# Last head's mean in full precision inside the output stage, and one unread full-precision matmul in the second layer's first feed-forward product

## The chip, the cores and the metric

The kernel runs on 1 core of a Trainium2 chip. The metric is the device time of one execution in microseconds. Before the change it is 868.81 us, the median of 3 runs (866.87 to 868.93).

## The reference

An encoder trunk of two layers works on 272 tokens (16 learned meta tokens and 256 given ones) of 1024 channels. Cut to what matters, one layer is:

```
u  = rms_norm(h)
q, k, v, g (retention), q, k, v (attention), gate_r, gate_a = split(u @ w_in)
r  = retention both ways, 8 heads of 128 values;
     per head: r / sqrt(mean(r*r) + 1e-6) * silu(g)      (r has its mean taken off)
y_r = r @ w_ret_o
y_a = windowed attention(q, k, v) @ w_att_o
h  = h + rms_norm((sigmoid(gate_r)*y_r + sigmoid(gate_a)*y_a) @ w_mix_o)
h  = h + rms_norm(square(relu(rms_norm(h) @ w_ff1)) @ w_ff2)
```

At the end the meta tokens are dropped. All of it is float32. The kernel computes a sigmoid as a tanh of half its argument, and 1/sqrt(x) as Exp(-0.5 Ln(x)) with one Newton step.

## The kernel before, in words

Channels lie on the 128 partitions and tokens on the free axis, so a product is 128 output channels by 272 tokens (layer 0) or 256 (layer 1, where the meta tokens' columns are no longer computed). `c0` is 0 or 16 for that. A product in float32 is made of three matmuls of a rounded type per 128 input channels (`mm3`, L135 to L138): high weights by high data, high by low, low by high. A full product (`product`, L146) is 8 such steps, 24 matmuls, into one bank of PSUM. The banks are named: three of tag a, two each of s and t, one of o. `wide()` (L85) deals out the tags in the rotation "asatats".

Weights arrive by DMA in units of 128 x 1024 (`unit`, L119). ScalarE copies a unit to its high part (L131), VectorE subtracts to get the low part (L132). 256 units pass through the kernel.

A layer runs in stages: the input projections; attention; retention; the attention output `att_o` (8 outputs of 4 steps, 12 matmuls each); the retention output `ret_o` (8 products); the mix (8 products) with a norm, `leave` (L296); the first feed-forward product `ff1` (32 products); the second. In layer 0 the second feed-forward product ends in `leave` too; layer 1 ends in a stage of its own, whose rows are normed in `scaled` (L834).

In the retention stage (L718 to L737) each head hh passes `similar` (decay weights by Exp, scores), `retained` (four full-precision instructions and a rounded one; a square on ScalarE; a split of the squares into high and low), and `normed` (L699): the mean of the squares over the head's 128 channels as two rounded matmuls with a matrix of 1/128 (`o128`, L702), then Ln, Exp (L705, L706), the Newton step, the gate, and a split into `rh` and `rl`, which `ret_o` reads. Between the heads' parts `fill(n)` puts n steps of the products gate_r and gate_a. Their results are added up on VectorE (`stt`, L92) into `thr` (one tile for all eight outputs) and `tha` (eight tiles). After the last head ScalarE computes the tanh of `thr` in one instruction of 8 x 256 elements and of `tha` in eight. `att_o` adds its results to 1 + tanh (tha) (L753), and `ret_o` to 1 + tanh(thr) in a similar manner.

The order of the instructions on each engine is made by the framework, which takes the code as traced and lists, engine by engine, what to issue next; the order in the code is a priority among those that are ready. Three means give the code a say. `tc.issue_after(x)` holds an instruction behind x where both are on one engine. `tc.keep_in_program_order(i)` holds i behind the instruction that was traced just before it on its engine. Tiles of a tag have a fixed number of buffers and wait for one. ScalarE computes Exp, Tanh and Ln from table sets: the compiler puts a table load before a function that isn't in the set loaded last, and `preload_act_table_set` (L207, L650, L743) loads a named set by hand.

The tanhs are held behind the last head's Exp:

```
        with tc.issue_after(last.ins):
            A.activation(thr[:, :, c0:], thr[:, :, c0:], AF.Tanh, scale=0.5)
            for x in tha:
                A.activation(x[:, c0:], x[:, c0:], AF.Tanh, scale=0.5)
        tc.keep_in_program_order(A.preload_act_table_set("natural_log_exp_and_others"))
```

`last` is the Exp of `normed(7)`. `mean` (L180) is a norm's mean over all 1024 channels, made of full-precision matmuls (L183) that take a float32 matrix as it is; `idle` is a 128 x 128 tile of zeros that `warm` (L175) uses.

Of the kernel before, what the change touches and what calls it, by code (L numbers as in the profile page):

```python
# [10 lines left out]
F32R = mybir.dt.float32r  # L11
F16 = mybir.dt.float16
BF16 = mybir.dt.bfloat16
AF = mybir.ActivationFunctionType
# [3 lines left out]
P = 128  # L18
# [4 lines left out]
T = SEQ + NM  # L23
# [18 lines left out]
def encoder(ctx: ExitStack, tc: tile.TileContext, order, w, h_in, gains, dec, decm, sink, sinkm, tabs, mats, esel, masks, rel, relm, grow, out):  # L42
    nc = tc.nc
    V, A, PE, G = nc.vector, nc.scalar, nc.tensor, nc.gpsimd
    mul, add, sub, mn = ALU.mult, ALU.add, ALU.subtract, ALU.min

    def pool(name, bufs=1, **kw):
        return ctx.enter_context(tc.tile_pool(name=name, bufs=bufs, **kw))
# [6 lines left out]
    four = pool("four", 4)  # L55
# [17 lines left out]
    def bank(tag, shape=None):  # L73
        t = psum.tile([P, 512], F32, tag=tag, name="ps_" + tag, bufs=BANKS[tag])
        if shape is None:
            return t
        n = int(np.prod(shape))
        v = t[:, :n]
        if len(shape) == 2:
            v = v.rearrange("p (a b) -> p a b", a=shape[0])  # L80
        elif len(shape) == 3:
            v = v.rearrange("p (a b c) -> p a b c", a=shape[0], b=shape[1])
        return v

    def wide():  # L85
        turn[0] += 1
        return "asatats"[turn[0] % 7]

    def f(t):
        return t.bitcast(F32)  # L90

    def stt(o, a, s, b, op0=mul, op1=mul):  # L92
        V.scalar_tensor_tensor(out=o, in0=a, scalar=s, in1=b, op0=op0, op1=op1)

    def split(xh, xl, x):
        A.activation(xh, x, AF.Copy)  # L96
        V.tensor_tensor(out=xl, in0=x, in1=f(xh), op=sub)  # L97

    def load(ap, dt=F32, name=None):
        t = const.tile(list(ap.shape), dt, name=name)  # L100
        nc.sync.dma_start(t, ap)
        return t
# [16 lines left out]
    def unit(*name):  # L119
        i = len(order)  # L120
        order.append(name)
        if not raws:
            list(fetch())
        raw, cuts = raws.pop(0)
        wh = ring.tile([P, D], F32R, tag="wh", name="wh")
        wl = ring.tile([P, D], F32R, tag="wl", name="wl")
        for c in cuts:
            with ExitStack() as later:
                for ins in held.get(i, ()):
                    later.enter_context(tc.issue_after(ins))  # L130
                A.activation(wh[:, c], raw[:, c], AF.Copy)  # L131
                V.tensor_tensor(out=wl[:, c], in0=raw[:, c], in1=f(wh[:, c]), op=sub)  # L132
        return wh, wl

    def mm3(ps, ah, al, bh, bl, first=True, last=True):  # L135
        PE.matmul(ps, ah, bh, start=first, stop=False)  # L136
        PE.matmul(ps, ah, bl, start=False, stop=False)  # L137
        return PE.matmul(ps, al, bh, start=False, stop=last)  # L138
# [3 lines left out]
    def flush():  # L142
        while deferred:
            deferred.pop(0)()

    def product(x, c0, tag, *name):  # L146
        wh, wl = unit(*name)
        ps = bank(tag, [T])
        for k in range(KD):
            sl = slice(k * P, (k + 1) * P)  # L150
            ins = mm3(ps[:, c0:], wh[:, sl], wl[:, sl], x[0][:, k, c0:], x[1][:, k, c0:], k == 0, k == KD - 1)
            if k == LAG and deferred:
                with tc.issue_after(ins.ins):
                    flush()
            yield ins, ps

    def proj(x, c0, tag, *name):
        for _, ps in product(x, c0, tag, *name):
            pass
        return ps  # L160
# [11 lines left out]
    idle = const.tile([P, P], F32, name="idle")  # L172
# [152 lines left out]
    mat = {}  # L325
# [37 lines left out]
    for l in range(DEPTH):  # L363
        c0 = 16 * l
        if l == 0:
            u, ss, early = lead()
        else:
            u, ss, _ = enter(l, 0, 0, update)
            early = [proj(u, 0, "asas"[i], "v_r", i) for i in range(4)]
        if l == 0:  # L370
            mat_sb = load(mats, name="mats")
            mat.update((n, mat_sb[:, i]) for i, n in enumerate(MATS))
            o128 = one.tile([P, P], F32R, tag="o128", name="o128")
# [124 lines left out]
        ao = tokens(5, "ao", (2, 4), 32 - c0)  # L498
# [3 lines left out]
        thr = slot(6, "thr")  # L502
# [46 lines left out]
        def behind():  # L549
            return tc.issue_after(anchor[0])  # L550
# [12 lines left out]
        if l == 0:  # L563
            ps = bank("s")
# [86 lines left out]
        tha = gate["gate_a"] = half("10a", "tha")  # L651
# [16 lines left out]
        sds, pos, pvs = {}, {}, {}  # L668
# [20 lines left out]
        def retained(hh):  # L689
            t = hh // 2  # L690
            po = pos[hh] = bank("ot"[hh % 2], [T])
            for c in range(2):
                PE.matmul(po[:, c0:], vr[:, c, hh * P:(hh + 1) * P], sds[hh][c][:, c0:], start=c == 0, stop=False)
            PE.matmul(po[:, c0:], vm[:, hh], tm[:, t, c0:], start=False, stop=True)
            sq = square(po[:, c0:], c0)
            pvs[hh] = four.tile([P, 2, T], F32R, tag="pt", name="sqs", bufs=3)
            split(*(pvs[hh][:, i, c0:] for i in range(2)), sq[:, c0:])

        def normed(hh):  # L699
            pv = bank("t", [T])  # L700
            for i in range(2):
                PE.matmul(pv[:, c0:], o128, pvs[hh][:, i, c0:], start=i == 0, stop=i == 1)  # L702
            y = two.tile([P, T], F32, tag="t1", name="vy")
            w2 = two.tile([P, T], F32, tag="t2", name="vw")
            A.activation(y[:, c0:], pv[:, c0:], AF.Ln, bias=eps)  # L705
            last = A.activation(y[:, c0:], y[:, c0:], AF.Exp, scale=-0.5)  # L706
            newton(w2[:, c0:], pv[:, c0:], 1e-6, y[:, c0:], w2[:, c0:])
            stt(w2[:, c0:], w2[:, c0:], -0.25, gt[:, hh, c0:])
            V.tensor_tensor(out=w2[:, c0:], in0=pos[hh][:, c0:], in1=w2[:, c0:], op=mul)
            split(rh[:, hh, c0:], rl[:, hh, c0:], w2[:, c0:])  # L710
            return last
# [6 lines left out]
        for hh in range(8):  # L718
            with behind():
                if hh < 7:  # L720
                    similar(hh + 1)
                retained(hh)
            fill(F[7])
            if hh == 0:
                for m in range(KD):
                    with tc.issue_after(ready.ins):
                        stt(gt[:, m, c0:], tg[:, m, c0:], 1.0, gt[:, m, c0:], op0=add)
                rh, rl = tokens(7, "rh", at=32 - c0), tokens(8, "rl", at=32 - c0)
            if hh % 2 and hh < 7:
                with behind():  # L730
                    meta((hh + 1) // 2)
            fill(F[6])
            with behind():
                last = normed(hh)
            fill(F[5])
        while queue or current:
            fill(1)  # L737

        with tc.issue_after(last.ins):
            A.activation(thr[:, :, c0:], thr[:, :, c0:], AF.Tanh, scale=0.5)  # L740
            for x in tha:
                A.activation(x[:, c0:], x[:, c0:], AF.Tanh, scale=0.5)
        tc.keep_in_program_order(A.preload_act_table_set("natural_log_exp_and_others"))  # L743

        for m2 in range(4):
            wh, wl = unit("att_o", m2)
            for i in range(2):
                m = 2 * m2 + i
                ps = bank(wide(), [T])
                for k in range(4):  # L750
                    sl = slice((4 * i + k) * P, (4 * i + k + 1) * P)
                    mm3(ps[:, c0:], wh[:, sl], wl[:, sl], ao[:, 0, k, c0:], ao[:, 1, k, c0:], k == 0, k == 3)
                stt(tha[m][:, c0:], tha[m][:, c0:], 1.0, ps[:, c0:], op0=add)  # L753

        z = tokens(2, "zh", at=32 - c0), tokens(3, "zl", at=32 - c0)
        for m in range(KD):
            ps = proj((rh, rl), c0, wide(), "ret_o", m)
# [16 lines left out]
        u, ss, accumulate = enter(l, 2, c0, update)  # L774
        fs, behind = [], []
# [8 lines left out]
        for m in range(KF):  # L784
            if m % KD == 0:
                a, b = ((5, 7), (8, 9), (6, 10), (2, 3))[m // KD]
                low = [tokens(i, "fl", (4,), 32 - c0) for i in ("10a", "10b")] if b == 10 else [tokens(b, "fl", at=32 - c0)]
                fs.append((rows(tokens(a, "fh", at=32 - c0)), sum(map(rows, low), [])))
            ps = proj(u, c0, wide(), "ff1", m)
            if l == 0 and 0 <= m - SUM < KD:  # L790
                accumulate(m - SUM)
            if l == 0 and m == SUM + KD:
                e2 = one.tile([P, T], F32, tag="rb", name="e2")
                A.activation(e2, mean([ss], c0), AF.Square, scale=8e-6 ** 0.5)
            behind.append((ps, fs[-1][0][m % KD][:, c0:], fs[-1][1][m % KD][:, c0:]))
            if len(behind) > BEHIND:
                squared(*behind.pop(0))
# [46 lines left out]
    for j in range(2):  # L844
# [22 lines left out]
        for i in range(2):  # L867
            sl = slice(j * 512, (j + 1) * 512)
# [6 lines left out]
    for i in range(2):  # L875
        for a, b in ((0, 512), (512, 768), (768, 1024)) if i else ((0, 512), (512, 1024)):
            sl = slice(a, b)
# [115 lines left out]
```

## Time and profile before

| what | value |
| --- | --- |
| median of 3 runs | 868.81 us (866.87 to 868.93) |
| profiled execution | 874.68 us |
| span of its trace | 872.9 us |
| mean granted TensorE clock | 0.996 |
| TensorE busy | 98% |
| VectorE busy | 70% |
| ScalarE busy | 65% |
| TensorE's share of the chain that ended last | 80% |
| VectorE's, ScalarE's share of it | 10%, 6% |

PE is TensorE's matmuls, PEld its weight loads, DVE VectorE, ACT ScalarE, POOL GpSimd and SP SyncE. The span is the time from the first to the last instruction; the profiled execution's own time has 1.8 us around it. The granted clock is a share of TensorE's full speed: 1.00 is 2.4 GHz and 0.50 is 1.2 GHz. Matmuls overlap: the duration of one (about 0.28 us) is longer than the step from its start to the start of the next, and the step is what counts. The chain that ended last is followed back from the last instruction to whatever released each.

### The profile page before, as it was taken

The numbers are of one execution on the slowest core, as the hardware profiler recorded it, in microseconds if no ns is written. First come the engines' busy times: TensorE is split into PE (matmuls) and PEld (weight loads), VectorE is DVE, ScalarE is ACT, GpSimd is POOL, SyncE is SP. The second block draws the span as 40 slices with busy tenths as digits, with TensorE's granted clock in tenths as the row PEclk, the third lists the DMA queues.
The fourth block names the chain that finished last, engine by engine and source line by source line (L and its number), as shares of the span: only waits on it lengthen the run. The fifth ranks groups of instructions, "written<-read, shape, count | busy, mean of one in ns | idle before, by whom it ended". The sixth has DMA issues, their size and how long they took to land.

```text
span 872.9 us, 16696 instructions
## 1 busy us (share of the span) xinstructions
PE 854.7 (98%) x6514; PEld 822.2 (94%) x6514; DVE 608.5 (70%) x1129; ACT 564.8 (65%) x1050; POOL 50.6 (6%) x114
## 2 busy tenths in 40 slices
PE   9999999999999999999999999999999999999997
PEld 8899999999989999999989999999999999998885
DVE  7889888878668555444468898888786775554544
ACT  7448788675558777544455578987845587783432
POOL 2112220000000000000000122200000000000000
PEclk9999999999999999999999999999999999999999
DMA  8544443446545655655635544434376276666661
GB/s 293 194 125 139 122 130 114 145 146 192 164 128 179 190 179 178 176 184 172 178 112 153 162 132 141 141 124 148 115 219 200 90 239 189 183 193 194 190 192 70
DMA packets 41407, 142.15 MB, mean 163 GB/s; under 512 B 5360, under 2 KB 6256, under 8 KB 41328
## 3 DMA queue, kind: packets, MB, share of 16 engines
q1 hardware_dynamic: 40896, 140.43, 52.3%
q8 instruction: 51, 0.84, 0.4%
q10 hardware_dynamic: 432, 0.66, 0.2%
q14 instruction: 28, 0.23, 0.1%
HBM read 140.02 MB, written 1.05 MB: 162 GB/s over the span
## 4 chain that ended last, share of the span: by engine, by line
PE 80%; DVE 10%; ACT 6%; issue 1%; DMA 1%; POOL 0%; SPq 0%; DVEq 0%; ACTq 0%; POOLq 0%
PE ps_a L136 12%; PE ps_a L137 12%; PE ps_a L138 12%; PE ps_s L138 5%; PE ps_s L136 5%; PE ps_s L137 5%; PE ps_t L136 4%; PE ps_t L137 4%; PE ps_t L138 4%; DVE wl L132 3%; PE ps_s L853 2%; PE ps_a L853 2%; PE ps_a L855 2%; PE ps_s L855 2%; PE ps_s L854 2%; PE ps_a L854 2%
## 5 line engine op out<-in xcount | busy, mean ns | idle before, releaser
L132 DVE TENSOR_TENSOR wl<-raw,wh 128x1024 fp32r<-128x1024 f32 x256 | 313.0, 1224 | 199.7 <-ACT wh L131 198.2
L131 ACT ACTIVATE wh<-raw 128x1024 fp32r<-128x1024 f32 x256 | 269.8, 1058 | 204.4 <-PE ps_a L137 62.3
L136 PE MATMUL ps_a<-uh,wh 128*128 128x272 f32 (+1 forms) x912 | 263.0, 289 | 2.8 <-ACT uh L242 2.8
L138 PE MATMUL ps_a<-uh,wl 128*128 128x272 f32 (+1 forms) x912 | 260.0, 285 | 0.5 <-DVE wl L132 0.3
L137 PE MATMUL ps_a<-ul,wh 128*128 128x272 f32 (+1 forms) x912 | 260.1, 286 | 0.0
L136 PEld LDWEIGHTS ps_a<-uh,wh 128*128 128x128 f32 x912 | 172.6, 189 | 3.8 <-ACT uh L242 3.2
L138 PEld LDWEIGHTS ps_a<-uh,wl 128*128 128x128 f32 x912 | 172.9, 190 | 1.2 <-DVE wl L132 0.8
L137 PEld LDWEIGHTS ps_a<-ul,wh 128*128 128x128 f32 x912 | 172.4, 189 | 0.4
L138 PE MATMUL ps_s<-uh,wl 128*128 128x272 f32 (+1 forms) x184 | 52.4, 285 | 0.3 <-DVE wl L132 0.3
L137 PE MATMUL ps_s<-ul,wh 128*128 128x272 f32 (+1 forms) x184 | 52.3, 284 | 0.0
L136 PE MATMUL ps_s<-uh,wh 128*128 128x272 f32 (+1 forms) x184 | 52.2, 284 | 0.0
L136 PE MATMUL ps_t<-uh,wh 128*128 128x272 f32 (+1 forms) x152 | 43.5, 286 | 1.3 <-ACT uh L242 1.3
L137 PE MATMUL ps_t<-ul,wh 128*128 128x272 f32 (+1 forms) x152 | 43.5, 286 | 0.0
L138 PE MATMUL ps_t<-uh,wl 128*128 128x272 f32 (+1 forms) x152 | 43.2, 284 | 0.0
L138 PEld LDWEIGHTS ps_s<-uh,wl 128*128 128x128 f32 x184 | 34.9, 190 | 0.5 <-DVE wl L132 0.5
L136 PEld LDWEIGHTS ps_s<-uh,wh 128*128 128x128 f32 x184 | 34.7, 189 | 0.0
L137 PEld LDWEIGHTS ps_s<-ul,wh 128*128 128x128 f32 x184 | 34.6, 188 | 0.0
L136 PEld LDWEIGHTS ps_t<-uh,wh 128*128 128x128 f32 x152 | 28.6, 188 | 1.5 <-ACT uh L242 1.5
L138 PEld LDWEIGHTS ps_t<-uh,wl 128*128 128x128 f32 x152 | 28.9, 190 | 0.0
L137 PEld LDWEIGHTS ps_t<-ul,wh 128*128 128x128 f32 x152 | 28.6, 188 | 0.1
L97 DVE TENSOR_TENSOR fl<-ft,fh 128x272 fp32r<-128x272 f32 (+1 forms) x64 | 27.6, 433 | 1.0 <-ACT fh L96 0.9
L96 ACT ACTIVATE fh<-ft 128x272 fp32r<-128x272 f32 (+1 forms) x64 | 27.2, 425 | 1.7
(311 smaller groups left out, 1963.5 us busy)
## 6 DMA issues: line engine op xcount, KB each, us to landing
raw<-in_w SPq DMA_DIRECT2D x256, 512.0 KB, 3.7
leads<-in_w SPq DMA_DIRECT2D x6, 256.0 KB, 5.6
tab<-in_tabs SPq DMA_DIRECT2D x2, 544.0 KB, 6.3
h<-in_h_in SPq DMA_DIRECT2D x3, 272.0 KB, 5.8
out<-yt SPq DMA_DIRECT2D x3, 256.0 KB, 2.1
leads<-in_w ACTq DMA_DIRECT2D x2, 256.0 KB, 3.4
gj<-in_grow SPq DMA_DIRECT2D x1, 512.0 KB, 4.7
mats<-in_mats SPq DMA_DIRECT2D x1, 320.0 KB, 7.2
```

The costliest lines, as they stand in the source:

```text
L96: A.activation(xh, x, AF.Copy)
L97: V.tensor_tensor(out=xl, in0=x, in1=f(xh), op=sub)
L131: A.activation(wh[:, c], raw[:, c], AF.Copy)
L132: V.tensor_tensor(out=wl[:, c], in0=raw[:, c], in1=f(wh[:, c]), op=sub)
L136: PE.matmul(ps, ah, bh, start=first, stop=False)
L137: PE.matmul(ps, ah, bl, start=False, stop=False)
L138: return PE.matmul(ps, al, bh, start=False, stop=last)
L853: PE.matmul(pss[i], xh, wh[:, sl], start=kk == 0, stop=False)
L854: PE.matmul(pss[i], xh, wl[:, sl], start=False, stop=False)
L855: PE.matmul(pss[i], xl, wh[:, sl], start=False, stop=kk == KF - 1)
```

## The change

It has six parts. For head 7 the squares aren't split, and the mean over them is one full-precision matmul (two instructions) with the float32 matrix `mat["o128"]`. `normed(7)` is taken out of the retention loop and traced in `att_o`, held behind the third matmul of step k = 1 of output 0; the tanhs of `tha` follow its Exp. `att_o` takes its banks from "asasa" and uses no bank of tag t. The tanh of `thr` is cut into three, for outputs 0 to 1, 2 to 4 and 5 to 7, traced behind the second, third and fourth unit of `att_o` and not held behind any instruction. The table preload is held behind the third of them. And in layer 1 a full-precision matmul of `idle` with 256 columns of the constant matrices goes to the bank of tag o, behind output 3 of `ff1`; nothing reads its result.

```diff
--- before.py
+++ after.py
@@ -693,13 +693,19 @@
                 PE.matmul(po[:, c0:], vr[:, c, hh * P:(hh + 1) * P], sds[hh][c][:, c0:], start=c == 0, stop=False)
             PE.matmul(po[:, c0:], vm[:, hh], tm[:, t, c0:], start=False, stop=True)
             sq = square(po[:, c0:], c0)
-            pvs[hh] = four.tile([P, 2, T], F32R, tag="pt", name="sqs", bufs=3)
-            split(*(pvs[hh][:, i, c0:] for i in range(2)), sq[:, c0:])
+            if hh == 7:
+                pvs[hh] = sq
+            else:
+                pvs[hh] = four.tile([P, 2, T], F32R, tag="pt", name="sqs", bufs=3)
+                split(*(pvs[hh][:, i, c0:] for i in range(2)), sq[:, c0:])
 
         def normed(hh):
             pv = bank("t", [T])
-            for i in range(2):
-                PE.matmul(pv[:, c0:], o128, pvs[hh][:, i, c0:], start=i == 0, stop=i == 1)
+            if hh == 7:
+                PE.matmul(pv[:, c0:], mat["o128"], pvs[hh][:, c0:], start=True, stop=True)
+            else:
+                for i in range(2):
+                    PE.matmul(pv[:, c0:], o128, pvs[hh][:, i, c0:], start=i == 0, stop=i == 1)
             y = two.tile([P, T], F32, tag="t1", name="vy")
             w2 = two.tile([P, T], F32, tag="t2", name="vw")
             A.activation(y[:, c0:], pv[:, c0:], AF.Ln, bias=eps)
@@ -730,27 +736,35 @@
                 with behind():
                     meta((hh + 1) // 2)
             fill(F[6])
-            with behind():
-                last = normed(hh)
+            if hh < 7:
+                with behind():
+                    normed(hh)
             fill(F[5])
         while queue or current:
             fill(1)
 
-        with tc.issue_after(last.ins):
-            A.activation(thr[:, :, c0:], thr[:, :, c0:], AF.Tanh, scale=0.5)
-            for x in tha:
-                A.activation(x[:, c0:], x[:, c0:], AF.Tanh, scale=0.5)
-        tc.keep_in_program_order(A.preload_act_table_set("natural_log_exp_and_others"))
+        def gates(ins):
+            with tc.issue_after(ins.ins):
+                last = normed(7)
+            with tc.issue_after(last.ins):
+                for x in tha:
+                    A.activation(x[:, c0:], x[:, c0:], AF.Tanh, scale=0.5)
 
         for m2 in range(4):
             wh, wl = unit("att_o", m2)
             for i in range(2):
                 m = 2 * m2 + i
-                ps = bank(wide(), [T])
+                ps = bank("asasa"[m % 5], [T])
                 for k in range(4):
                     sl = slice((4 * i + k) * P, (4 * i + k + 1) * P)
-                    mm3(ps[:, c0:], wh[:, sl], wl[:, sl], ao[:, 0, k, c0:], ao[:, 1, k, c0:], k == 0, k == 3)
+                    ins = mm3(ps[:, c0:], wh[:, sl], wl[:, sl], ao[:, 0, k, c0:], ao[:, 1, k, c0:], k == 0, k == 3)
+                    if m == 0 and k == 1:
+                        gates(ins)
                 stt(tha[m][:, c0:], tha[m][:, c0:], 1.0, ps[:, c0:], op0=add)
+            if m2:
+                x = thr[:, (0, 0, 2, 5)[m2]:(0, 2, 5, 8)[m2], c0:]
+                A.activation(x, x, AF.Tanh, scale=0.5)
+        tc.keep_in_program_order(A.preload_act_table_set("natural_log_exp_and_others"))
 
         z = tokens(2, "zh", at=32 - c0), tokens(3, "zl", at=32 - c0)
         for m in range(KD):
@@ -786,7 +800,11 @@
                 a, b = ((5, 7), (8, 9), (6, 10), (2, 3))[m // KD]
                 low = [tokens(i, "fl", (4,), 32 - c0) for i in ("10a", "10b")] if b == 10 else [tokens(b, "fl", at=32 - c0)]
                 fs.append((rows(tokens(a, "fh", at=32 - c0)), sum(map(rows, low), [])))
-            ps = proj(u, c0, wide(), "ff1", m)
+            for ins, ps in product(u, c0, wide(), "ff1", m):
+                pass
+            if l and m == 3:
+                with tc.issue_after(ins.ins):
+                    tc.keep_in_program_order(PE.matmul(bank("o", [T])[:, c0:], idle, mat_sb[:, 0:2].rearrange("p a b -> p (a b)"), start=True, stop=True))
             if l == 0 and 0 <= m - SUM < KD:
                 accumulate(m - SUM)
             if l == 0 and m == SUM + KD:
```

## Rows read from the trace of the kernel before

**Rows 1.** Busy time of each engine, its share of the span, and instructions.

```profile
PE 854.7 (98%) x6514; PEld 822.2 (94%) x6514; DVE 608.5 (70%) x1129; ACT 564.8 (65%) x1050; POOL 50.6 (6%) x114
```

**Rows 2.** Retention stages by windows: length, busy (instructions) per engine, clock, DMA share, GB/s.

```profile
134.00:161.00 27.00, 26.68 (x202) 25.80 (x202) 26.07 (x60) 21.40 (x49) 0.00 (x0) 1.00 0.45 135
573.00:600.00 27.00, 27.00 (x218) 26.53 (x217) 26.45 (x60) 20.93 (x48) 0.00 (x0) 1.00 0.49 156
```

**Rows 3.** Timeline of PE: start, length, engine, line, output<-inputs, tile, [idle before].

```profile
697.46 0.28 PE L136 MATMUL ps_a<-uh,wh 128*128 128x256 f32 x1
...
700.29 0.28 PE L136 MATMUL ps_t<-uh,wh 128*128 128x256 f32 x1
...
585.18 0.28 PE L136 MATMUL ps_a<-uh,wh 128*128 128x256 f32 x1
...
587.56 0.28 PE L702 MATMUL ps_t<-sqs,o 128*128 128x256 f32 x1
...
193.47 0.37 PE L136 MATMUL ps_t<-ao,wh 128*128 128x272 f32 x1
193.68 0.29 PE L137 MATMUL ps_t<-ao,wh 128*128 128x272 f32 x1
...
626.45 0.28 PE L137 MATMUL ps_a<-ao,wh 128*128 128x256 f32 x1
626.82 0.39 PE L136 MATMUL ps_t<-ao,wh 128*128 128x256 f32 x1
```

**Rows 4.** Timeline of PE around the mean in the feed-forward product of layer 0.

```profile
307.24 0.62 PE L183 MATMUL ps_o<-ss,mats 128*128 128x272 f32 x2
...
307.82 0.28 PE L137 MATMUL ps_a<-ul,wh 128*128 128x272 f32 x1
```

**Rows 5.** Timeline of PE and ACT at two instructions written later in the code.

```profile
280.60 0.29 PE L136 MATMUL ps_t<-uh,wh 128*128 128x272 f32 x1
...
256.16 0.41 ACT L222 ACTIVATE sq<-h 128x272 f32<-128x272 f32 x1
...
556.57 0.51 ACT L674 ACTIVATE tt<-rel,de 128x256 f32<-128x256 f16 x1
```

**Rows 6.** Timeline of DVE and ACT in layer 1's retention stage.

```profile
570.22 0.42 DVE L93 SCALAR_TENSOR_TENSOR thr<-ps_a,rb 128x256 f32<-128x256 f32 x1
...
594.53 0.42 DVE L93 SCALAR_TENSOR_TENSOR thr<-ps_a,rb 128x256 f32<-128x256 f32 x1
...
595.68 0.46 ACT L705 ACTIVATE vy<-ps_t,eps 128x256 f32<-128x256 f32 x1
```

**Rows 7.** Timeline of ACT behind the last head's Exp in layer 1.

```profile
622.35 0.42 ACT L706 ACTIVATE vy<-vy 128x256 f32<-128x256 f32 x1
622.79 1.28 ACT L740 ACT_TABLE_LOAD   x1
624.08 1.92 ACT L740 ACTIVATE thr<-thr 128x2048 f32<-128x2048 f32 x1
...
626.21 2.56 ACT L742 ACTIVATE tha<-tha 128x256 f32<-128x256 f32 x8
```

**Rows 8.** Timeline of ACT and PE at the mix norm of layer 1 and the tail.

```profile
682.05 0.38 ACT L189 ACTIVATE y<-ps_o 128x256 f32<-128x256 f32 x1 [0.42 <-PE ps_o L183]
...
685.51 0.38 PE L136 MATMUL ps_t<-uh,wh 128*128 128x256 f32 x1 [1.27 <-ACT uh L242]
...
867.19 0.29 ACT L838 ACTIVATE y<-ysum,ex 128x1 f32<-128x1 f32 x1
```

**Rows 9.** Timeline of ACT at the first norm and at tg of layer 1.

```profile
465.93 0.38 ACT L189 ACTIVATE y<-ps_o 128x272 f32<-128x272 f32 x1
...
564.94 1.28 ACT L649 ACT_TABLE_LOAD   x1
```

**Rows 10.** Windows of the start, columns as in rows 2.

```profile
40.00:42.00 2.00, 0.82 (x5) 0.52 (x4) 1.97 (x4) 0.97 (x3) 1.24 (x2) 1.00 0.60 174
44.00:46.00 2.00, 2.00 (x11) 2.00 (x10) 0.77 (x3) 0.99 (x1) 0.00 (x0) 0.50 0.46 174
```

## The prediction, made before the changed kernel was run

> **What bounds the kernel now.** I read the busy table first. TensorE (PE) is busy 98% of the span, ScalarE (ACT) 65%, VectorE (DVE) 70% [rows 1]; the chain of waits is PE for 80%, so time is gained only if PE waits less or steps faster, and lost wherever another engine makes PE wait. Then the stretches: in the retention stage of each layer PE stays at 26.68 and 27.00 of 27 us, but with DVE at 26.07 and 26.45 and ACT at 21.40 and 20.93 [rows 2]. That is the stage with the least slack: DVE can't catch up once it is made late, and ACT has only 27 - 21.40 = 5.6 us and 27 - 20.93 = 6.1 us to give. The reader should keep these two numbers.
>
> The timeline of PE, taken from start to start, shows that the same matmul has two steps at a granted clock of 1.00. Layer 1: 24 matmuls of output projection 697.46 to 700.29, 117.9 ns each; 21 matmuls 585.18 to 587.56, 113.3 ns each [rows 3]. In layer 0, with 272 columns, 24 matmuls of a product read the same way take 126.7 ns each before 251 and 123.3 ns after. A stretch keeps its step until a wait or a matmul of another kind. All of the first feed-forward product of layer 1 (694.9 to 776.6, 694 matmuls), 405 matmuls from 633.0 and 455 in layer 0 from 193.7 are in the slow step. The last begins at a matmul that waits for bank t (193.47 to 193.68, 211 ns [rows 3]).
>
> **The change, part by part.**
>
> *Head 7's mean.* Gone: in each layer one ACT copy and one DVE subtraction of the squares. Added: two full-precision instructions in place of two rounded ones. The only row of one such mean: two of them and the next matmul pair, 307.24 to 307.82, 0.58 us for 272 columns [rows 4]; less one ordinary step of 0.12 that is 0.46, against about 0.25 for the two steps now. +0.2 a layer, +0.4 in all; bounds 0 (if the next product would have waited) and 0.92 (0.46 twice and nothing saved).
>
> *The unread matmul.* Two instructions of 256 columns; by the same row 0.46 x 256/272 = 0.43, +0.45 with its load; bounds 0.2 and 0.6. What it can bring is the fast step for the rest: after a full-precision matmul followed at once by an ordinary product the settled step was fast in 8 of 9 places in layer 1 and in all of some 20 in layer 0; after head 7's two rounded ones it is slow. 28 products remain, 672 matmuls x (117.8 - 113.3 = 4.4 ns) = 2.96. I take -2.96 + 0.45 = -2.5; bounds +0.6 (no flip) and -2.8.
>
> *att_o without bank t.* The wait at 193.47 (211 ns, 0.09 too long) and its twin in layer 1 (matmul 626.45 to 626.82, 0.37, 0.25 too long [rows 3]) go. What could be late next is a bank whose reader waits for head 7's chain: the first reuse of a bank of att_o is output 5's, 60 matmuls or 6.8 us after its start, and the first reader needs the later mean (0.7 + 0.5), Ln and Exp (0.9), a table load and a tanh (1.28 + 0.32 [rows 7]): 3.7 us. 3 us of cover; cost 0, bounds 0 and 1. In the stretch att_o to mix the fast step would give 455 x 3.4 ns = 1.55 and 405 x 4.4 = 1.78; since ACT and DVE stalls (below) reset the step, I take half: -1.7, bounds 0 and -3.8 with the two waits.
>
> *The three tanhs of thr and the table preload.* This decides. The tanh of thr was held behind head 7's Exp; its pieces now have no hold at all, and the preload follows only the last of them. The trace shows what this program does with an instruction that has operands and no hold: it goes where its engine first has room, whatever stands before it in the code. A square written behind the ninth feed-forward product, whose first matmul is at 280.60, runs at 256.16; the decay Exp of layer 1's retention runs at 556.57, ahead of the tanh of tg that stands before it and whose table load starts at 564.94 [rows 5, 9]. thr 0 to 1 are complete at 570.22 + 0.42, the last at 594.53 + 0.42 [rows 6]. So I forecast that the tanhs run inside the retention stage, between the heads' Ln and Exp (the Ln of head 3 is at 595.68 [rows 6]).
>
> There each costs table loads, which the compiler puts before a function that isn't in the loaded set. That Ln and Exp share a set only where the code names it is my reading of the code: behind each tanh it names that set by hand (lines 650, 743), which would be needless if a demand found it. So I count one load before the first tanh, two for each of heads 0 to 3 (Ln, then Exp), one at the preload: 10 x 1.28 [rows 7] = 12.8, and the 1.92 of the tanh in three pieces, about 2.2. 15.0 us more ACT per layer against the idle 5.6 to 6.1: 9 over. DVE's work waits behind it and has no room to recover. I take 7.5 of it on the path per layer, **+15**; bounds 0 (PE's other products cover all) and 15 a layer.
>
> The Trainium skill speaks to both assumptions in "ScalarE: Activation LUTs". Its section "Table sets: the hidden batching unit" lists Ln, then Exp, as one load, since one set has both; no row here shows a demand for Ln without the preload, so this is rival R2b below. Its section "What ACT_TABLE_LOAD costs" adds to the load a drain of about its length. Here the trace disagrees: an Exp ends at 622.77, the load runs 622.79 to 624.07 and the tanh starts at 624.08 [rows 7].
>
> *After that.* The tanhs of tha, behind head 7's Exp, need one load and have no preload behind them, so Ln and Exp of each later norm switch. Leave of mix in both layers and of the second feed-forward in layer 0: Ln at 682.05 has 0.42 idle before it, Exp follows at once, and PE's gap ends on this chain [rows 8]; 1.28 - 0.42 = 0.86 for the load before Ln and 1.28 for the one before Exp, 2.1 each, **+6.4** (bounds 2 and 8). The norm at the start of layer 1 (Ln at 465.93, PE working beside it): **+1.3**, bounds 0 and 2.6. The tail: Ln and Exp at 867.19, nothing beside them [rows 8]: 2 x 1.28 = **+2.6** (bounds 1.3 and 2.6). The tanh of tg in layer 1 finds its set there, so the load at 564.94 [rows 9] goes: **-1.0**, bounds 0 and -1.3.
>
> *The clock.* After PE had only 0.82 of 2 us busy (40 to 42) the granted clock fell, and was 0.50, the 1.2 GHz level, in 44 to 46 [rows 10]; 16 matmuls there stepped at 227 ns instead of 123, 1.7 us. The gap before 685.51 is 1.27 now [rows 8] and would be 3.4; one of three such gaps may do it: **+1.7**, bounds 0 and 5.
>
> **The sum**: 15 + 6.4 + 1.3 + 2.6 + 1.7 + 0.4 - 2.5 - 1.7 - 1.0 = +22.2. The profiled execution took 874.68, span 872.9 and 1.8 around it; 874.68 + 22.2 = 896.9. It lies 5.9 above the median of 868.81, so on the median 891.0. With terms at their bounds, not all together, 877 to 903.
>
> **Rivals.**
>
> *R1, the other side: the order holds as written, and the steps flip.* If the list of ACT leaves the tanhs behind att_o (what rows 5 show to move are pieces of 0.4 to 0.5 us; nothing of a tanh's length was seen to move), the kernel has the same loads as now and only PE counts: 1.55 + 1.78 + 2.96 for the fast step, 0.19 for 44 slow matmuls after 621.4, 0.09 + 0.25 for the waits on bank t, and 0.16 for the wait on a weight at 632.6: 6.98, less 0.4 and 0.45: -6.1, **862.7**. It decides at one point: whether a tanh of thr starts before head 7's mean. For it: the steps after full-precision matmuls. Against it: rows 5.
>
> *R2: the tanhs move, but the stage swallows them.* ACT's 6 us, and the fact that PE has products of gate_a to run whatever the heads do; if the last pieces come late, few heads switch. Then A is near 0 and 22.2 - 15 = 7.2 remain: **876**. Against it: DVE at 26.45 of 27 [rows 2].
>
> *R2b: they move, and one load serves Ln and Exp.* Then a stage has 6 loads (one before each tanh piece, one back): 7.7 + 2.2 = 9.9, less 5.9 idle is 4.0; of that the same share, 3.3 a layer, 6.7. Of the leaves only the first Ln in each layer loads (0.86 each, 1.7), start and tail nothing, the clock 1.0: 6.7 + 1.7 + 1.0 + 0.4 - 2.5 - 1.7 = 5.6: **874**. Against it: lines 650 and 743 as read above.
>
> *R3: it doesn't do what it says.* The order holds and the steps stay: +0.85 and the 0.5 of waits off: **869**. Only 8 of 9 and 20 of 20 speak against it.
>
> **How the numbers follow.** Forecast 0.54 (slower), R1 0.22 (faster), R2 0.11 and R2b 0.08 (slower), R3 0.05 (same). A difference within 0.3% (2.6 us) can't be told from no change here. Faster 0.22, same 0.05, slower 0.73. As cases of both signs count, the range goes from 861 to 903; the forecast's own is 877 to 903.
>
> **What would show it.** A tanh of thr before 600 in layer 1 and before 165 in layer 0, with some 20 table loads more in all; PE with gaps in 573 to 600 instead of 27.00 of 27; a load between Ln and Exp at each leave and in the tail. Step of PE behind the fourth product: 113 ns. Wrong, if thr's tanhs stand at att_o: then the first step of the argument fails and R1 decides; if they moved and PE still is at 26.5 or more of 27 in the stage, R2; Ln and Exp behind one load, R2b.

## The result, and the profile after

The changed kernel takes 899.87 us (median of 4, 899.55 to 900.6) against 868.76 us for the kernel before (now also a median of 4): ratio 1.0364, 95% interval 1.0348 to 1.0381. The forecast was 891.0 in a range of 861 to 903. Sign and main cause came out as forecast; the loss is 31.1 us where 22.2 was forecast, and two terms of the sum were wrong.

The busy table of the changed kernel answers to [rows 1]. ACT has 34.8 us more work, and PE's share falls by two points.

```profile
PE 860.9 (96%) x6516; PEld 826.6 (92%) x6516; DVE 609.2 (68%) x1127; ACT 599.6 (67%) x1081; POOL 52.5 (6%) x114
```

The windows of the two retention stages answer to [rows 2] (columns as there; layer 1 now begins this stage 15 us later). Look at ACT first: from 21.40 and 20.93 busy it went to 26.81 and 26.59 of 27, full. DVE went down, from 26 to 21: it waits. PE lost 2.1 and 3.0 us of busy time, and the clock column of layer 0 shows 0.94.

```profile
134.00:161.00 27.00, 24.57 (x167) 23.01 (x166) 21.30 (x49) 26.81 (x47) 0.00 (x0) 0.94 0.38 117
586.00:613.00 27.00, 24.03 (x189) 22.81 (x188) 20.43 (x47) 26.59 (x47) 0.00 (x0) 1.00 0.40 117
```

The timeline of ACT in layer 0's stage (start, length, engine, line, output<-inputs) shows what fills it. L766 is the tanh of thr, L711 Ln, L656 and L712 Exp, L767 the preload. The first tanh runs at 137.87, 59 us ahead of the attention output that it stands in, and a load stands before it and then, until the preload at 173.13, before each Ln and before the first Exp behind each Ln. The second and third tanh come behind an Exp (152.16 and 169.28) and have no load of their own.

```profile
136.58 1.28 ACT L766 ACT_TABLE_LOAD   x1
137.87 0.66 ACT L766 ACTIVATE thr<-thr 128x544 f32<-128x544 f32 x1
138.55 1.28 ACT L711 ACT_TABLE_LOAD   x1
139.85 0.49 ACT L711 ACTIVATE vy<-ps_t,eps 128x272 f32<-128x272 f32 x1
140.35 1.28 ACT L656 ACT_TABLE_LOAD   x1
...
167.04 1.28 ACT L712 ACT_TABLE_LOAD   x1
...
173.13 1.28 ACT L767 ACT_TABLE_LOAD   x1
```

There are ten loads in each stage, as forecast, and 38 in the kernel where there were 9. The prediction wrote of some 20 more; its own terms come to 27. PE's timeline shows where it stops: at a head's mean (L708), for late squares in the first row and for a late step of VectorE on `vw` in the second, with [idle before <- releaser].

```profile
154.39 0.39 PE L708 MATMUL ps_t<-sqs,o 128*128 128x272 f32 x1 [2.09 <-ACT sqs L96]
...
622.43 0.36 PE L708 MATMUL ps_t<-sqs,o 128*128 128x256 f32 x1 [2.66 <-DVE vw L93]
```

Behind such a stop the clock falls. In these windows (columns as in rows 2) PE is busy 0.31 and 1.59 of 2 us, and then the granted clock is 0.53 and 0.62 for 4 us of full work, partly at the 1.2 GHz level.

```profile
152.00:154.00 2.00, 0.31 (x3) 0.09 (x1) 2.00 (x6) 2.00 (x6) 0.00 (x0) 1.00 0.16 64
154.00:156.00 2.00, 1.59 (x10) 1.38 (x11) 1.99 (x6) 1.98 (x6) 0.00 (x0) 1.00 0.29 33
156.00:158.00 2.00, 2.00 (x12) 2.00 (x11) 1.39 (x2) 1.97 (x3) 0.00 (x0) 0.53 0.61 229
158.00:160.00 2.00, 2.00 (x11) 1.96 (x11) 0.63 (x3) 1.99 (x4) 0.00 (x0) 0.62 0.81 242
```

At the mix norm of layer 1 the chain of [rows 8] now has two loads in it. Ln waits for one, which starts where the copy ahead of it ends, and Exp for the other; PE's gap grew from 1.27 to 3.43.

```profile
701.75 1.28 ACT L189 ACT_TABLE_LOAD   x1
703.04 0.38 ACT L189 ACTIVATE y<-ps_o 128x256 f32<-128x256 f32 x1
703.44 1.28 ACT L190 ACT_TABLE_LOAD   x1
704.74 0.42 ACT L190 ACTIVATE y<-y 128x256 f32<-128x256 f32 x1
...
707.78 0.38 PE L136 MATMUL ps_t<-uh,wh 128*128 128x256 f32 x1 [3.43 <-ACT uh L242]
```

And in the tail:

```profile
890.63 1.28 ACT L856 ACT_TABLE_LOAD   x1
891.92 0.29 ACT L856 ACTIVATE y<-ysum,ex 128x1 f32<-128x1 f32 x1
892.24 1.28 ACT L857 ACT_TABLE_LOAD   x1
893.53 0.20 ACT L857 ACTIVATE y<-y 128x1 f32<-128x1 f32 x1
```

Lastly the unread matmul (L807). The 24 matmuls of a product behind it, 723.74 to 726.57, step at 117.9 ns; those ahead of it at 113.5 (20 steps from 715.38 to 717.65). It was to bring the fast step and brought the slow one.

```profile
715.38 0.28 PE L136 MATMUL ps_t<-uh,wh 128*128 128x256 f32 x1
...
717.65 0.28 PE L136 MATMUL ps_t<-uh,wh 128*128 128x256 f32 x1
...
720.49 0.59 PE L807 MATMUL ps_o<-mats,idle 128*128 128x256 f32 x2
720.73 0.47 PE L136 MATMUL ps_a<-uh,wh 128*128 128x256 f32 x1
...
723.74 0.28 PE L136 MATMUL ps_s<-uh,wh 128*128 128x256 f32 x1
...
726.57 0.28 PE L136 MATMUL ps_a<-uh,wh 128*128 128x256 f32 x1
```

### The profile page after: what moved, and what is told of

Read it like the earlier page. It is cut to its first block, busy times and chain, and to the rows that moved or that the text cites. A ratio compares the mean times of both kernels' runs of the same rounds, so it can differ in the third digit from the quotient of the medians.

```text
span 898.8 us, 16736 instructions
## 1 busy us (share of the span) xinstructions
PE 860.9 (96%) x6516; PEld 826.6 (92%) x6516; DVE 609.2 (68%) x1127; ACT 599.6 (67%) x1081; POOL 52.5 (6%) x114
## 4 chain that ended last, share of the span: by engine, by line
PE 73%; ACT 13%; DVE 10%; issue 2%; DMA 1%; POOL 0%; SPq 0%; DVEq 0%; ACTq 0%; POOLq 0%
PE ps_a L136 11%; PE ps_a L138 11%; PE ps_a L137 11%; PE ps_s L136 4%; PE ps_s L137 4%; PE ps_s L138 4%; PE ps_t L136 4%; PE ps_t L137 4%; PE ps_t L138 4%; DVE wl L132 3%; ACT wh L131 2%; PE ps_a L872 2%; PE ps_a L871 2%; PE ps_a L873 2%; ACT L711 1%
## 5 line engine op out<-in xcount | busy, mean ns | idle before, releaser
L136 PE MATMUL ps_t<-uh,wh 128*128 128x272 f32 (+1 forms) x168 | 48.6, 292 | 7.0 <-ACT uh L242 7.0
L138 PE MATMUL ps_s<-uh,wl 128*128 128x272 f32 (+1 forms) x176 | 50.1, 285 | 0.0
L137 PE MATMUL ps_t<-ul,wh 128*128 128x272 f32 (+1 forms) x168 | 48.7, 290 | 0.0
L138 PE MATMUL ps_t<-uh,wl 128*128 128x272 f32 (+1 forms) x168 | 48.6, 289 | 0.0
L136 PEld LDWEIGHTS ps_t<-uh,wh 128*128 128x128 f32 x168 | 32.9, 197 | 7.4 <-ACT uh L242 7.4
L137 PE MATMUL ps_a<-fl,wh 128*128 128x272 f32 x128 | 36.7, 287 | 0.0
L136 PE MATMUL ps_a<-fh,wh 128*128 128x272 f32 x128 | 36.7, 287 | 0.0
L138 PE MATMUL ps_a<-fh,wl 128*128 128x272 f32 x128 | 36.7, 287 | 0.0
L137 PEld LDWEIGHTS ps_t<-ul,wh 128*128 128x128 f32 x168 | 32.6, 194 | 0.0
```

## The experiments

Stage times below are differences between the first matmuls of two stages in the PE timeline. The retention stage runs from head 0's first matmul in `retained` to the first of the attention output.

### The kernel before once more

No edit.

> The kernel before once more, unchanged, for a second trace of it. Theory: the profiled execution of 874.68 stands 5.9 above the timed ones because TensorE's step (113 or 118 ns for 256 columns) falls differently from one execution to the next, so this trace has another span (866 to 874) and other stretches in the slow step, with the same order of instructions. Rival: the steps are fixed by the program, so the same stretches (the whole first feed-forward product of layer 1 among them) are slow again, and the profile is merely long somewhere else. Timed against the kernel before: no difference, ratio 0.998 to 1.002.

Ratio 0.9988 (0.9968 to 1.0008). Its trace has a span of 866.4 us, 6.5 less than the first one. Nearly all of that (6.3) is PE's step: the first feed-forward product of layer 1 took 89.68 us instead of 92.76, retention output and mix of layer 1 0.86 and 0.85 less, three stages of layer 0 0.24, 0.64 and 0.64 less. The same product as in [rows 3] steps at (699.43 - 696.71) / 24 = 113.3 ns here:

```profile
696.71 0.28 PE L136 MATMUL ps_t<-uh,wh 128*128 128x256 f32 x1
...
699.43 0.28 PE L136 MATMUL ps_a<-uh,wh 128*128 128x256 f32 x1
```

So the step isn't fixed by the program. The profiled execution on which the prediction was built happened to have the slow step in all of these stretches, and that is why it stood 5.9 over the median. The rest of this section measures against this second trace where it uses stage times.

### The three tanhs held

```diff
             with tc.issue_after(last.ins):
                 for x in tha:
-                    A.activation(x[:, c0:], x[:, c0:], AF.Tanh, scale=0.5)
+                    ins = A.activation(x[:, c0:], x[:, c0:], AF.Tanh, scale=0.5)
+            return ins
...
-                        gates(ins)
+                        tanhs = gates(ins)
...
-                A.activation(x, x, AF.Tanh, scale=0.5)
+                with tc.issue_after(tanhs.ins):
+                    A.activation(x, x, AF.Tanh, scale=0.5)
```

> The changed kernel, but the three tanhs of thr are held behind the last tanh of tha, so that they run in the attention output and the table preload follows them. Theory (the early tanhs and the lost preload make the whole loss; the moved full-precision mean, the banks and the unread matmul cost under 1 us together): 862 to 869, no more than 0.2% over the kernel before, 4 table loads fewer than 10 in all (9 as before), retention stages back at 57.4 and 54.6 us. Rival (the moved mean and its chain hold up the attention output, or the new banks do): 875 or more, with the loss in the stretch from the attention output to the mix.

871.29 us, ratio 1.0026 (1.0011 to 1.0042): 9 loads, stages of 57.12 and 54.39 us. One missing order on three instructions (and the preload that goes with them) made 28.6 of the 31.1 us. The time lies above the 862 to 869 that were expected; the run after next names the place of the remaining 0.26%.

### The preload alone put right

```diff
             with tc.issue_after(last.ins):
                 for x in tha:
                     A.activation(x[:, c0:], x[:, c0:], AF.Tanh, scale=0.5)
+            tc.keep_in_program_order(A.preload_act_table_set("natural_log_exp_and_others"))
```

> The changed kernel with one more table preload, pinned behind the last tanh of tha in each layer; the tanhs of thr still run early. Theory: the loads before Ln and Exp of the norms and in the tail go (12 loads less, 3 more: 9 net), which gives back the tail's 2.4, some 4 at the start of layer 1, and 1.5 to 2 at each of three norms: 899.9 - 12 = 888 (885 to 891); the retention stages stay 6.7 us longer each. Rival (the loss behind the retention stages comes from the granted clock falling in gaps that are there anyhow, or from the slow step): 896 or more.

886.18 us: 13.7 us back, within the expected range. Of its trace against the changed kernel's: 2.15, 2.15 and 2.17 at the three norms behind mix and second feed-forward product, 2.46 in the tail, and 1.92, 4.32 and 0.85 in the stretches right behind those norms and at the start of layer 1. These add up to 16.0, and 14.1 of them are left in the span: the start has a fall of the clock that the changed kernel's trace lacks (1.25 more), and layer 1's retention stage is 0.9 longer. The retention stages stayed long (63.97 and 62.20 us). So the loss splits into 14 us behind the stages and 15 us in them.

### The held version without the unread matmul

```diff
-            if l and m == 3:
-                with tc.issue_after(ins.ins):
-                    tc.keep_in_program_order(PE.matmul(bank("o", [T])[:, c0:], idle, mat_sb[:, 0:2].rearrange("p a b -> p (a b)"), start=True, stop=True))
```

> As e1_held, without the unread full-precision matmul in layer 1's first feed-forward product. Theory of the prediction (a full-precision matmul followed by an ordinary product sets the fast step of 113 ns): this is 2.5 us slower than e1_held, its feed-forward product in the slow step of 118 ns throughout. Rival (the step settles anew behind every interruption, either way, by how it falls there: in the changed kernel 70 matmuls before the unread one went at 113 ns and the 671 behind it at 118): not slower than e1_held, and faster by 3.4 us (0.45 and 671 x 4.4 ns) where the product starts in the fast step.

868.91 us, ratio 1.0002 (0.9983 to 1.002), 2.4 under the held version. The feed-forward product took 89.67 us instead of 93.18. What is left of the change (the full-precision mean moved into the attention output, the other banks, the three tanhs at their new places) is worth nothing that can be measured: in the trace the retention stages are 0.28 and 0.15 shorter than in the second trace of before, and attention and retention output together 0.72 and 0.72 longer.

### Early work without its loads

Squares in place of tanhs, so that no table is asked for; the tanh of thr is left out.

```diff
             if m2:
                 x = thr[:, (0, 0, 2, 5)[m2]:(0, 2, 5, 8)[m2], c0:]
-                A.activation(x, x, AF.Tanh, scale=0.5)
-        tc.keep_in_program_order(A.preload_act_table_set("natural_log_exp_and_others"))
+                A.activation(x, x, AF.Square, scale=0.5)
```

with the preload behind the tanhs of tha, as in the run with the preload put right.

> The changed kernel with its three early pieces as squares in place of tanhs (this leaves out the tanh of thr) and the preload behind tha's tanhs: as much early work for ScalarE in the same places, but no table load in the retention stages. Theory (the loads make the loss there): the stages 57.4 and 54.6 us again (within 0.7), the whole 870 to 873. Rival (the tanhs' own 2.2 us or their places ahead of the heads' work make it): the stages still 60 or more, the whole 876 to 886.

872.24 us, stages of 57.00 and 54.01 us. The windows of [rows 2] in this kernel: as many early instructions, and PE is not held up.

```profile
134.00:161.00 27.00, 26.84 (x206) 26.15 (x206) 26.04 (x58) 22.76 (x51) 0.00 (x0) 1.00 0.48 137
573.00:600.00 27.00, 27.00 (x221) 26.59 (x219) 25.64 (x58) 21.96 (x49) 0.00 (x0) 1.00 0.53 159
```

Early work of the same length in the same places costs nothing; the loads are the loss in these stages.

### More loads

A preload behind each early tanh, on top of the run with the additional preload. The last piece's preload stays.

```diff
-        tc.keep_in_program_order(A.preload_act_table_set("natural_log_exp_and_others"))
...
                 A.activation(x, x, AF.Tanh, scale=0.5)
+                tc.keep_in_program_order(A.preload_act_table_set("natural_log_exp_and_others"))
```

> The run with the additional preload behind tha, and in it a preload behind each of the three early tanhs instead of the last alone: these fall so that the two retention stages have 18 and 15 table loads where they had 10 each (46 in all for 31). Theory (the loads on a ScalarE with no idle time left are the loss): 13 more x 1.28 = 16.6 us more work there, of which the share of the first run (6.6 to 7.7 of 9 us) to all of it comes onto the path: 886.2 + 12 to 17 = 898 to 903. Rival (the loss comes from the first switches at a few heads and further loads are hidden): 886 to 892.

894.06 us, 7.9 more than with 10 loads a stage. Neither expectation held: the theory's 12 to 17 is too much, the rival's ceiling of 892 too low. (In the traces the whole kernels have 42 and 29 loads; the difference of 13 is as expected.) Layer 0's stage went from 57.00 (no load, the run with squares) to 63.97 (10) and 69.25 (18), layer 1's from 54.01 to 62.20 (10) and 65.14 (15): 0.70 and 0.66 a load in layer 0, 0.82 and 0.59 in layer 1, of the 1.28 that a load takes, falls of the clock included. The further loads cost no more each than the first ten: it is not that ACT's idle time is used up first and all of the rest is paid. No run has between 0 and 10 loads, so whether the first few are free is not shown.

### The unread matmul alone, and what sets the step

Five kernels are the kernel before with one unread full-precision matmul in layer 1's first feed-forward product and nothing else of the change.

```diff
-            ps = proj(u, c0, wide(), "ff1", m)
+            for ins, ps in product(u, c0, wide(), "ff1", m):
+                pass
+            if l and m == 3:
+                with tc.issue_after(ins.ins):
+                    tc.keep_in_program_order(PE.matmul(bank("o", [T])[:, c0:], idle, mat_sb[:, 0:2].rearrange("p a b -> p (a b)"), start=True, stop=True))
```

> The kernel before with the unread matmul alone. Theory (this matmul sets the slow step behind it each time, as in the three traces of kernels that have it): the 671 matmuls behind it at 118 ns whatever the ones ahead of it do; the time at the upper end of the kernel before, 871.5 to 873 with a narrow spread, ratio 1.001 to 1.005. Rival (the step falls by chance behind each interruption and three times slow was chance): 113 ns here, 866 to 869.

In the second the condition is `l and m == 3 and k == 3`, inside the loop.

> The kernel before with the unread matmul one half product earlier: behind the fourth step of output 3 of the first feed-forward product instead of behind its last. Theory (a full-precision matmul within a product sets the fast step, as behind the moved mean in the attention output; between two products, where the bank changes, the slow one): 113 ns behind it, 866.5 to 868.5. Rival (the place does not matter, these operands set the slow step): 118 ns, 871.5 to 873.

In the third, the operands are others:

```diff
-idle, mat_sb[:, 0:2].rearrange("p a b -> p (a b)"), start=True
+mat["o128"], f(u[0][:, 0, c0:]), start=True
```

> The kernel before with the unread matmul at its place, but of the matrix of 1/128 and the normed input's high part in place of zeros and a constant. Theory (the place decides): 118 ns behind it as with zeros, 871.5 to 873. Rival (the operands decide): 113 ns, 866.5 to 868.5.

In the last two each operand is changed back by itself: `idle, f(u[0][:, 0, c0:])`, and `mat["o128"], mat_sb[:, 0:2].rearrange("p a b -> p (a b)")`.

> The kernel before with the unread matmul of zeros (as in the change) and the normed input's high part (as in the run with real operands). Theory (the moving operand decides: one that was the constant matrices set the slow step, one that is the normed input the fast one): 113 ns behind it, 867.4 to 869.5. Rival (the stationary operand decides, zeros set the slow step): 118 ns, 871 to 873.5.

> The kernel before with the unread matmul of the matrix of 1/128 and the constant matrices as the change has them. Theory (the moving operand decides): 118 ns behind it, 871 to 873.5. Rival (the stationary operand decides): 113 ns, 867.4 to 869.5. If this and the run with zeros and the normed input go the same way, neither operand alone decides.

| stationary, moving operand; place | median us | ratio, 95% interval | step behind |
| --- | --- | --- | --- |
| zeros, constants; behind the product | 872.49 | 1.0035 (1.002 to 1.005) | 117.8 |
| zeros, constants; within it | 872.13 | 1.0017 (0.9998 to 1.0036) | 117.8 |
| zeros, normed input; behind it | 872.89 | 1.0041 (1.0025 to 1.0057) | 117.8 |
| 1/128, normed input; behind it | 868.92 | 0.9994 (0.9978 to 1.001) | 113.3 |
| 1/128, constants; behind it | 869.06 | 0.9992 (0.9976 to 1.0008) | 113.3 |

The stationary operand decides. The rows of PE with the normed input moving, first with zeros, where a product takes 700.00 - 697.17 = 2.83 us:

```profile
693.92 0.59 PE L793 MATMUL ps_o<-uh,idle 128*128 128x256 f32 x2
...
697.17 0.28 PE L136 MATMUL ps_t<-uh,wh 128*128 128x256 f32 x1
...
700.00 0.28 PE L136 MATMUL ps_a<-uh,wh 128*128 128x256 f32 x1
```

then with the matrix of 1/128, 2.72 us:

```profile
696.20 0.59 PE L793 MATMUL ps_o<-uh,mats 128*128 128x256 f32 x2
...
699.37 0.28 PE L136 MATMUL ps_t<-uh,wh 128*128 128x256 f32 x1
...
702.09 0.28 PE L136 MATMUL ps_a<-uh,wh 128*128 128x256 f32 x1
```

All eight traces of kernels with zeros have the slow step behind them: six in which the last steps ahead were fast, two in which they were slow. So zeros bring the slow step whatever the step was. The three traces with 1/128 (these two and that of the next run) have the fast step behind; in these two it was fast ahead too, and only in the next run's did it turn, from 117.8 to 113.3. The traces without an unread matmul have either. That 1/128 brings the fast step rests on that one trace, and in the medians it brings nothing against the kernel before.

The place and the moving operand are ruled out, and the theories of the second to the fifth run fell with them; that of the first held, its median too (871.5 to 873 expected), but not the narrow spread: 870.55 to 875.09. One thing was changed together with the values: the zeros lie in the tile `idle`, the 1/128 in that of the constant matrices. No run puts zeros elsewhere, so value and tile are not told apart.

### Both stretches with the fast step

The unread matmul of 1/128 and normed input in the feed-forward product, and a second one in layer 1:

```diff
-            ps = proj((rh, rl), c0, wide(), "ret_o", m)
+            for ins, ps in product((rh, rl), c0, wide(), "ret_o", m):
+                pass
+            if l and m == 0:
+                with tc.issue_after(ins.ins):
+                    tc.keep_in_program_order(PE.matmul(bank("o", [T])[:, c0:], mat["o128"], f(rh[:, 0, c0:]), start=True, stop=True))
```

> The kernel before with two unread full-precision matmuls of real operands in layer 1: behind the first product of the retention output (1/128 matrix, the heads' high part) and behind the fourth of the first feed-forward product (1/128 matrix, normed input). Theory (both set the fast step; without them the stretches of 405 and 694 matmuls fall either way from one execution to the next): 866.5 to 868.8, below the kernel before by 0.1 to 0.3% and with fewer executions over 870. Rival (only the one place works, the other sets the slow step or none): 869 to 871.

870.07 us, ratio 1.0007 (0.9991 to 1.0023). The times fit the rival's 869 to 871, the trace the theory: 113.3 ns in both stretches and a span of 866.4. But the timed executions spread from 867.49 to 873.17 as those of the kernel before do. So the fast step was had in the one execution seen, and no gain in the times. Either the step doesn't stay so in each execution, or the spread of the kernel before comes from elsewhere; only a profiled execution shows the step, and this stays open. No kernel tried here beats the kernel before beyond the measurement.

## Why the prediction was right or wrong, point by point

**The order.** Right. The tanhs without a hold ran in the retention stages, between the heads' Ln and Exp; the rival in which the order holds (R1) falls with the first row of ACT above. Held, the kernel is back at 871.

**Two loads for Ln and Exp.** Right. 138.55 and 140.35 are a load each for Ln and the Exp behind it; at the mix norm of layer 1 it is 701.75 and 703.44. R2b falls: the Trainium skill's page "ScalarE: Activation LUTs", section "Table sets: the hidden batching unit", has one load for Ln, then Exp; here that is so only where the code names the joint set.

**The load's price by itself.** Right: 1.28, and the next instruction starts 1.29 to 1.30 behind the load's start in each of the rows above (136.58 and 137.87, 138.55 and 139.85). The drain that the same page of the Trainium skill adds in "What ACT_TABLE_LOAD costs" is in none of them.

**+15 in the retention stages.** The size is right: 6.77 and 6.82 us against the second trace of before, 7.5 each forecast. The step that led to it failed, so the size is in part luck. It took 15.0 us more ACT work less 5.6 to 6.1 idle and put 7.5 of the remaining 9 on the path. But that idle time is of a window of 27 us, and the stage is twice as long. The whole stage of layer 0, in the second trace of before and in the changed kernel (columns as in rows 2):

```profile
133.16:190.54 57.38, 57.07 (x430) 55.17 (x429) 50.72 (x110) 42.33 (x89) 0.00 (x0) 1.00 0.47 139
132.48:196.63 64.15, 59.83 (x428) 56.70 (x427) 50.70 (x109) 54.38 (x98) 0.00 (x0) 0.97 0.41 124
```

ACT had 57.38 - 42.33 = 15.1 us idle there (13.1 in layer 1), took on 12.1 more (10.8), and still has 9.8 (9.2). So it is not out of time over the stage; it is nearly full only while the loads run (36.7 of the 37.8 us from 136.6 to 174.4), and the loss comes where they hold up a head. By the squares and the further loads a load costs 0.6 to 0.8 us. The loss is made of two parts that the term did not name: in layer 0 4.0 us more PE idle, nearly all before a head's mean, and 1.7 of clock; in layer 1 4.8 and 1.7. (The clock's part is busy time x (1 - granted clock), summed over windows of 1 us.)

**+6.4 at the three norms, +2.6 in the tail.** Right: 2.15, 2.15 and 2.17, and 2.45.

**+1.3 - 1.0 for the start of layer 1, +1.7 for the clock.** This is the term that was mis-sized. The forecast had one more fall of the clock, behind one of three longer gaps at norms. A fall came with all three, and the trace has six in all: one in each retention stage, one behind each of the three norms, and one behind the stop at the first norm of layer 1. That of the mix norm of layer 0 cost 2.65 us, the others 1.7 each, 11.2 together; the kernel before has one, of 1.7, at 43 to 47, which the changed kernel's trace lacks. Each PE gap of over 3 us at a norm brought a fall, at 261.92 while the gap still lasted and at 463.31 and 709.07 behind it, and none of the gaps of 1.3 to 1.4 there in the kernel before. The length of a gap alone does not tell: in the retention stage of layer 1 a gap of 1.63 was followed by a fall in the run with the preload put right (588.58 and 589.77), and one of 1.65 in the changed kernel (596.98) by none. Against the second trace of before, 1.9 (first feed-forward product of layer 0), 4.1 (the projections of layer 1, two falls) and 0.9 (layer 1's feed-forward product, beside the unread matmul) came behind the norms: 6.9 where 2.0 was forecast. The windows of the worst show PE idle first, then the clock at 0.50:

```profile
260.00:262.00 2.00, 0.00 (x0) 0.00 (x0) 1.19 (x3) 1.96 (x4) 0.00 (x0) 0.98 0.00 0
262.00:264.00 2.00, 0.56 (x2) 0.56 (x3) 2.00 (x7) 0.97 (x3) 0.00 (x0) 0.50 0.00 0
264.00:266.00 2.00, 2.00 (x11) 2.00 (x10) 2.00 (x6) 1.57 (x4) 0.00 (x0) 0.50 0.00 0
```

**-2.5 for the unread matmul.** Wrong in sign. The step that failed is "after a full-precision matmul followed at once by an ordinary product the settled step was fast": the places counted for it had values of the heads or matrices of the norms stationary, this one zeros. By the traces it costs 3.4 us against the fast step (93.08 against 89.68 us), and in the medians of the three runs with zeros and nothing else 1.9 to 3.6 us against the kernel before.

**-1.7 for the attention output to the mix.** Seen in the trace, and no gain. The stretch has the fast step in the changed kernel (113.3 ns, 473 matmuls), and so has the second trace of before for most of it. The term was worked out against an execution in which these stretches were slow.

**The balance.** From the second trace of before to the changed kernel the span grew by 898.8 - 866.4 = 32.4 us, 10.2 more than the sum had: 5.9 for the unread matmul (-2.5 became +3.4), 4.9 for the clock and the start of layer 1, 1.9 for the attention output to the mix (+0.2), less 1.4 in the retention stages and some 1 of small terms (0.7 of it at the start, without the fall at 43 to 47).

**The moved mean and the banks.** +0.4 and 0 were forecast; the run without tanhs early and without the unread matmul is at 1.0002. Two slips in these terms change nothing: 117.8 - 113.3 is 4.5, not 4.4, and the bound of -3.8 adds up to -3.7.

## What to carry to other kernels

An instruction moved later in the code, and freed of its hold, does not move later by that: here it ran about when its operands were there. If it pushes out a table set that its new neighbours share, each of them pays a load until the set is named again. By these stages, count a load on an engine that is full around it at about half to two thirds of its length, as an estimate, and a load on a norm's chain in full. Look for a fall of the clock behind each gap of TensorE that grows: here all three that went from 1.3 or 1.4 us to 3.4 or 3.5 brought one, of 1.7 to 2.65 us. Read an engine's idle time over the whole stage and not in one window of it. Before building on what one profiled execution shows (here a step of 118 for 113 ns), look at how that execution stands to the median, and take a second trace.

## What the runs showed of the hardware that was not expected

A full-precision matmul whose stationary operand is all zeros, with ordinary matmuls following at once, left these at 117.8 ns a step for some 670 matmuls, in eight traces of eight; with a matrix of 1/128 in its place they ran at 113.3 ns, in three of three, at the same granted clock of 1.00. Whether it is the values or the tile that holds them is not told apart, and why a stationary operand should set the step of later matmuls is not explained by any run here.
